# Two pairs of convolution-gate tiles by seven quarter products, with the attention work moved ahead of them

## The chip, the cores and the metric

The kernel runs on one core of one Trainium2 chip. A core has a matmul engine (TensorE, PE in the profile; its weight loads are PEld), a vector engine (VectorE, DVE), a scalar engine (ScalarE, ACT), GpSimd (POOL), and SyncE (SP), which issues most DMAs. The metric is the device time of one execution in microseconds. The kernel before takes 994.15 us (median of three runs, 994.03 to 994.83).

## The reference

One decoder layer over a prompt of 512 tokens and 64 sample tokens (8 sequences of 8), all in float32, width 1024. Cut to what the change touches:

```
h = rmsnorm(x, norm1_g) * (1 + sc1) + sh1
proj = h @ w_in                      # columns: B, C, x (1024 each), q, k, v, gates ga, gb
u = c_gate * xa                      # C * x
uc, new_conv = causal_conv(u, conv_buf, conv_w)      # width 3
ya = (b_gate * uc) @ w_conv_out
o = attend(q, k, v, sinks)           # window 128, 4 kv heads of 64, 16 query heads, ALiBi, sinks
yb = o @ w_attn_out
mixed = sigmoid(ga) * ya + sigmoid(gb) * yb
x = x + g1 * (mixed @ w_mix_out)     # then norm, ConvFFN, residual, final norm
```

`sc1, sh1, g1, ...` come from `silu(c) @ w_ada + b_ada`. Prompt and sample tokens share the weights. The prompt attends to its own previous 128 positions; a sample sequence attends to a cache of 128 keys and its own 8.

## The kernel before

**Layout.** Activations lie transposed, channels on the 128 partitions and the 512 + 64 tokens along the row, eight such tiles for 1024 channels. A column tile of a weight is 1024 x 128, loaded as one tile `raw` of 128 x 8 x 128 (512 KB). float32 is kept by splitting: `hi` is the operand rounded to a short format, by ScalarE (`whi<-raw` for weights), and `lo` the rest, by VectorE (`wlo<-raw,whi`). A product is then hi x hi + hi x lo + lo x hi. `product` (line 228) does one column tile: 8 k-steps, each three passes over two token groups of 256 and 320, which is 48 matmuls into one of two double PSUM tiles `mm`.

**Pairs.** `pair_product` (line 367) does two column tiles at once by seven products of a quarter in place of eight (each of 4 k-steps, three passes, 288 tokens: 84 matmuls). Its operands are sums and differences of halves: of weights in `pair_weights` (316), which gives steps `sums1`, `ah`, `al` and so on that `in_turn` (362) hangs behind the parts of the pair before; of activations in `PairOperands` (255) with `sums`, `high`, `low`, `n3`. In before the two gates (eight pairs, `sigmoid_pair`, 1245), the mixing product and the FFN use pairs; the convolution's B, C, x do not.

**The order of the work around the change.** First the queries and keys of head 0, then the convolution loop over eight channel tiles m: products C(m), x(m), B(m), written below as C0, x0, b0. C times x goes into `pad`, GpSimd copies state out of it, ScalarE and VectorE make the three taps `y`, and `conv_times` multiplies B by `y` into `cy`, which is split into `gh`, `gl`. In rounds m = 1 to 3 `key_parts` and `queries` (805) of the next heads stand ahead of C(m). `queries` makes a product, splits it, and moves its low half to the other 64 partitions by GpSimd's DMA queue (`q<-low`, line 821). Then `state_out`, eight products with `w_conv_out` (`conv_out`), the eight gate pairs, the products with `w_attn_out`, and the rest.

**The filler.** Smaller work is written as a generator and set between k-steps: `tick` (201) adds a rate for each k-step, and for each whole number one step of the generator is issued. Through the convolution loop it is `beside_conv` (1200): first `attention` (1062), 16 pieces (4 heads x 4 blocks of 128 tokens). Round n issues the values of piece n-2 (`prompt_values`, copied out by ScalarE at line 1057 as `o<-aux`), the transposes of piece n-1 (`prompt_turn`, copied at 1040) and the scores of piece n (`prompt_scores`), then the softmax (890: VectorE, and ScalarE's exponentials at 900). `prompt_ready` holds a head's first round back until eight k-steps after its queries. Decode follows for two quarters of the cache (`decode_scores`, `decode_values`), then `modulation(2048)` (1156): four groups of 16 small matmuls (`aux<-ada,cT`, line 1149) from eight loads `ada` of 256 KB each. Its loads go on SP's queue, in order with the weights.

**Who sets the order.** TensorE runs in program order throughout. The other engines' orders are set by a scheduler that estimates durations, until the line `pinned += [pe, act, dve]` ahead of the gates, from which ScalarE and VectorE are in program order too. Pools limit what can be early: four `raw`, five each of `whi` and `wlo`, 57 slots of a general pool, four PSUM banks `aux` for all small products, two double banks `mm`. In `w_split_adding` (168), used in before for six weights of the FFN, the low part is made by ScalarE (minus the high part) and a DMA of GpSimd's queue that adds `raw`.

Of the kernel before, what the change touches and what calls it, by code (L numbers as in the profile page):

```python
# [16 lines left out]
P = 128  # L17
# [12 lines left out]
Q_TICKS = 8  # L30
CACHE_AT = 15, 16
EPS = 1e-6
NEG = -1e33
# [38 lines left out]
def step_kernel(ctx: ExitStack, tc: tile.TileContext, ins: dict, outs: list):  # L72
# [57 lines left out]
    def sv(t):  # L130
        return t[:, 512:576]
# [795 lines left out]
    def decode_scores(q, s, cV):  # L927
# [38 lines left out]
        yield False  # L966

    def decode_values(q, s, cV):
        pt = []
        for kt in range(2):  # L970
# [7 lines left out]
            pt.append(t)  # L978
            yield False
        yield False  # L980
        c = slice(512 + 32 * q, 512 + 32 * q + 32)
        for j in range(2):
            O = aux()
            matmul(O, vt(4)[:, j * P : j * P + P], pt[1], start=True, stop=False)
            p4 = pt[0].rearrange("p (h b r) -> p h b r", h=4, b=4)
            o4 = O.rearrange("p (h b r) -> p h b r", h=4, b=4)
            for b in range(4):
                matmul(
                    o4[:, :, b, :], cV[b // 2][:, b % 2, j * P : j * P + P], p4[:, :, b, :],
                    start=False, stop=(b == 3),  # L990
                )
            oX = slot("oX", shape=[P, 2, 32])
            for hf in range(2):
# [9 lines left out]
                nc.sync.dma_start(dst[HALF[1 - hf]], oX[HALF[hf]])  # L1003
            yield False

# [56 lines left out]
    def attention():  # L1062


        scored = turned = None
        for n in range(18):
            arg = (n // 4, n % 4) if n < 16 else None
# [14 lines left out]
            yield False  # L1082
        filler[1] = 0.5
        waiting = None
# [114 lines left out]

    def beside_conv():  # L1200
# [6 lines left out]
    gcv = []  # L1207
    for m in range(NK):
        if m in (5, 6):
# [21 lines left out]
        nc.scalar.copy(c_sb, ps)  # L1231
        ps = product(weights(kpm(w_in, 2048 + m * P), NK), h)
        u = padded()
# [5 lines left out]
        y = conv(u, parT[:, 64 + m : 65 + m], parT[:, 72 + m : 73 + m], parT[:, 80 + m : 81 + m], stT[:, m, :])  # L1239
        ps = product(weights(kpm(w_in, m * P), NK), h)  # L1240
        gcv.append(split_slot(conv_times(ps, y), "g"))
    state_out(NK, ncv_p[:], ncv_s[:])
# [22 lines left out]

    ya, made = [], {}
    wco, wao = ins["w_conv_out"][0], ins["w_attn_out"][0]
    gate_cols = [c + m * P for c in (4608, 5632) for m in range(0, NK, 2)]
# [17 lines left out]
    w_last = weights(kpm(wco, (NK - 1) * P), NK)  # L1286
    gate_raws(0)
    pinned += [pe, act, dve]
    w, steps = pair_weights(*raws[0])
    steps = in_turn(steps)  # L1290
    for n in sorted(steps):
        steps[n]()
    gate_raws(1)
    conv_out(NK - 1, w_last)
    drain()
    sg, o = [], []
    w_next = {}

# [10 lines left out]
    for n in range(len(gate_cols)):  # L1309
# [7 lines left out]
        else:  # L1317
# [636 lines left out]
```

## Time and profile before

| | us |
|---|---|
| median of three runs | 994.15 (994.03 to 994.83) |
| profiled execution | 995.13 |
| its span | 993.4 |
| TensorE busy, share | 977.9, 98% |
| VectorE busy, share | 688.8, 69% |
| ScalarE busy, share | 464.6, 47% |
| GpSimd busy, share | 103.7, 10% |
| granted TensorE clock, mean | 0.996 |

The span is what the profiler saw from the first to the last instruction; the execution's own time lies 1.7 us above it. In the trace the convolution loop runs from 65 to 323 us, the products with `w_conv_out` to 382, the gate pairs to 471 and the products with `w_attn_out` to 532. Helpers record every operation under one line (111 in before, 112 in after), so groups are told apart by the names of their tiles: `mm<-hh,whi` is a pass of a product of the activations h, `aux<-kh,q` are prompt scores, `aux<-ident,s` transposes of softmax rows, `aux<-pt,V` values. Idle time in the list of waits is put down to what came last. A matmul's records overlap, since the engine is pipelined, so what one costs is read from start to start.

### The profile page before, as it was taken

Reading aid. Unit: us, or ns where it says so; the run is one execution under the profiler, and the core shown is the slowest. Engines: PE = TensorE matmul, PEld = TensorE weight load, DVE = VectorE, ACT = ScalarE, POOL = GpSimd, SP = SyncE. Lnnn points to the kernel's source line nnn. Section 1 sums busy time; section 2 is a strip of 40 time slices with the busy share of each in tenths; the row PEclk is TensorE's granted clock in tenths of the full one; section 3 lists DMA queues with packets and bytes.
Section 4 is the critical chain, followed back from the end, with each engine's and each line's share of the span. In section 5 each row is a group of like instructions: output and inputs, shape, how many; then the busy total and the mean of one; then the engine's idle time right before and its main releaser. Section 6 shows DMA issues by size and latency. Waiting matters only on the chain.

```text
span 993.4 us, 18735 instructions
## 1 busy us (share of the span) xinstructions
PE 977.9 (98%) x7492; PEld 939.1 (95%) x7492; DVE 688.8 (69%) x1289; ACT 464.6 (47%) x861; POOL 103.7 (10%) x275
## 2 busy tenths in 40 slices
PE   7999999999999999999999999999999999999997
PEld 5899999999999989999889999999999999999997
DVE  5736776676452348888578778896569994579853
ACT  5454555555334325454334468653225552245453
POOL 2221101020100000000000032111001110001120
PEclk9999999999999999999999999999999999999999
DMA  9984332243422753234962543433232232323302
GB/s 298 320 245 113 85 87 74 86 116 108 145 68 65 238 191 86 85 86 129 342 221 70 146 110 85 108 102 91 85 107 85 86 89 83 107 77 100 101 10 96
DMA packets 174345, 122.33 MB, mean 123 GB/s; under 512 B 6983, under 2 KB 160942, under 8 KB 173970
## 3 DMA queue, kind: packets, MB, share of 16 engines
q1 hardware_dynamic: 170242, 109.36, 36.3%
q0 software_dynamic: 3872, 11.51, 4.6%
q8 instruction: 59, 0.97, 0.4%
q14 instruction: 28, 0.23, 0.1%
q10 hardware_dynamic: 144, 0.26, 0.1%
HBM read 109.17 MB, written 7.35 MB: 117 GB/s over the span
## 4 chain that ended last, share of the span: by engine, by line
PE 88%; DVE 4%; DMA 3%; issue 2%; ACT 1%; SPq 0%; POOL 0%; POOLq 0%; DVEq 0%; ACTq 0%
PE mm L111 63%; PE aux L111 22%; PE aux L1049 2%; PE aux L1149 1%; DMA ad<-in_w_ada 1%; DVE wlo L111 1%; DMA wlo<-raw 1%; DMA raw<-in_w_in 1%; SPq L418 0%; DVE uv L111 0%; DVE raw L111 0%; DVE y L111 0%; DVE cy L111 0%; ACT whi L111 0%; DVE fl L111 0%
## 5 line engine op out<-in xcount | busy, mean ns | idle before, releaser
L111 ACT ACTIVATE whi<-raw 128x1024 fp32r<-128x1024 f32 (+2 forms) x166 | 170.2, 1034 | 150.6 <-PE mm L111 80.6
L111 DVE TENSOR_TENSOR wlo<-raw,whi 128x1024 fp32r<-128x1024 f32 (+2 forms) x160 | 190.4, 1193 | 47.3 <-ACT whi L111 46.8
L111 PE MATMUL mm<-hh,whi 128*128 128x256 f32 (+2 forms) x560 | 124.7, 299 | 0.6 <-ACT hh L111 0.6
L111 PE MATMUL mm<-hh,wlo 128*128 128x256 f32 (+2 forms) x560 | 121.8, 294 | 0.0
L111 PE MATMUL mm<-hl,whi 128*128 128x256 f32 (+2 forms) x560 | 121.1, 295 | 0.0
L111 PEld LDWEIGHTS mm<-hh,whi 128*128 128x128 f32 x560 | 93.1, 188 | 2.9 <-ACT hh L111 1.2
L111 PEld LDWEIGHTS mm<-hh,wlo 128*128 128x128 f32 x560 | 94.2, 188 | 0.0
L111 PEld LDWEIGHTS mm<-hl,whi 128*128 128x128 f32 x560 | 93.6, 188 | 0.4 <-DVE hl L111 0.4
L111 PE MATMUL mm<-th,whi 128*128 128x288 f32 x224 | 66.6, 297 | 0.4 <-DVE uv L111 0.4
L111 PE MATMUL mm<-th,wlo 128*128 128x288 f32 x224 | 66.1, 295 | 0.0
L111 PE MATMUL mm<-tl,whi 128*128 128x288 f32 x224 | 66.0, 295 | 0.0
L111 PE MATMUL mm<-fl,whi 128*128 128x256 f32 (+1 forms) x304 | 65.2, 295 | 0.0
L111 PE MATMUL mm<-fh,whi 128*128 128x256 f32 (+1 forms) x304 | 64.8, 295 | 0.3 <-DVE rt L111 0.3
L111 PE MATMUL mm<-fh,wlo 128*128 128x256 f32 (+1 forms) x304 | 65.0, 295 | 0.0
L111 DVE SCALAR_TENSOR_TENSOR x<-mm,modT,x 128x512 f32<-128x512 f32 (+1 forms) x29 | 19.6, 676 | 57.7 <-PE mm L111 57.7
L111 PEld LDWEIGHTS mm<-fh,whi 128*128 128x128 f32 x304 | 50.8, 188 | 0.5 <-PE mm L111 0.5
L111 PEld LDWEIGHTS mm<-fl,whi 128*128 128x128 f32 x304 | 50.9, 188 | 0.0
L111 PEld LDWEIGHTS mm<-fh,wlo 128*128 128x128 f32 x304 | 50.9, 188 | 0.0
L900 ACT ACTIVATE s<-s,nmx 128x256 f32<-128x256 f32 (+1 forms) x72 | 34.0, 475 | 32.0 <-DVE nmx L897 31.2
L111 PE MATMUL aux<-2h,whi 128*128 128x288 f32 (+2 forms) x160 | 47.3, 296 | 0.0
L111 PE MATMUL aux<-2l,whi 128*128 128x288 f32 (+2 forms) x160 | 47.3, 295 | 0.0
L111 PE MATMUL aux<-2h,wlo 128*128 128x288 f32 (+2 forms) x160 | 47.2, 295 | 0.0
(332 smaller groups left out, 2610.7 us busy)
## 6 DMA issues: line engine op xcount, KB each, us to landing
raw<-in_w_in SPq DMA_DIRECT2D x52, 512.0 KB, 4.2
raw<-in_w_up SPq DMA_DIRECT2D x44, 512.0 KB, 3.9
ada<-in_w_ada SPq DMA_DIRECT2D x64, 256.0 KB, 5.7
ad<-in_w_ada SPq DMA_DIRECT2D x32, 256.0 KB, 6.3
raw<-in_w_down SPq DMA_DIRECT2D x16, 512.0 KB, 3.6
raw<-in_w_conv_out SPq DMA_DIRECT2D x8, 512.0 KB, 3.5
raw<-in_w_attn_out SPq DMA_DIRECT2D x8, 512.0 KB, 4.7
raw<-in_w_mix_out SPq DMA_DIRECT2D x8, 512.0 KB, 5.1
```

The source lines that it names most:

```text
L111: done = getattr(self.engine, name)(*args, **kwargs)
L900: nc.scalar.activation(s[x // 2][:, x % 2, :w], s[x // 2][:, x % 2, :w], AF.Exp, bias=nmx[:, x : x + 1], accum_out=den[:, x : x + 1],)
L1049: done = nc.tensor.matmul(O[HALF[par], :256], vt(i - nkt + 1 + kt)[:, hd * 64 : hd * 64 + 64], pts[kt][:, par * 256 : par * 256 + 256], st ...
L1149: done = nc.tensor.matmul(ps[32 * j : 32 * j + 32, :], cT[:, k, :], cols[k][j], start=(k == 1), stop=(k == NK - 2),)
```

## The change

- B's last four column tiles (m = 4 to 7) leave the loop. They are made after it as two pairs by `pair_product`: `b_pair`. Their `y` are kept until then. The pair operands of h, which before were made beside `conv_out`, are made in the loop, m = 4 to 7, and their last part in the first B pair.
- Attention's rate is 0.24 for 0.19, decode's 0.35 for 0.5; the rest of both is issued at the end of the loop, ahead of the pairs. Between a piece's scores and its transposes there is one more round. `key_parts` and `queries` of the next heads stand between C(m) and x(m), m = 0 to 2. x's weights are prepared ahead of the copy of C.
- In the convolution loop weights from C3 on (eleven) take their low parts by `w_split_adding`.
- `decode_scores` issues both halves of a quarter in one step. `decode_values` uses for each of its two outputs only the half of the columns that belongs to it, in one bank, in one step.
- ScalarE and VectorE are in program order from the B pairs on. The weights of `w_conv_out` are prepared two products ahead, the weight steps of the first gate pair are spread over `conv_out` m = 3 to 6, and `modulation(2048)` moves from there to beside the gate pairs, its rest issued before the last of these.

```diff
+ATT_RATE, ADDING_FROM, B_PAIRS = 0.24, 3, (4, 6)
...
 decode_scores
-            for hf in range(2):
-                hd = 2 * j + hf
+        for j in range(2):
+            for hf in range(2):
+                hd, at = 2 * j + hf, j * 256
...
-            yield False
+        yield False
...
 decode_values
+        O = aux()
         for j in range(2):
-            O = aux()
-            matmul(O, vt(4)[:, j * P : j * P + P], pt[1], start=True, stop=False)
+            hs = slice(2 * j, 2 * j + 2)
+            own = slice(j * 256, j * 256 + 256)
+            matmul(O[:, own], vt(4)[:, j * P : j * P + P], pt[1][:, own], start=True, stop=False)
             for b in range(4):
                 matmul(
-                    o4[:, :, b, :], cV[b // 2][:, b % 2, j * P : j * P + P], p4[:, :, b, :],
+                    o4[:, hs, b, :], cV[b // 2][:, b % 2, j * P : j * P + P], p4[:, hs, b, :],
...
 attention
-        for n in range(18):
+        for n in range(19):
...
-            turned = (*scored[:2], prompt_turn(*scored)) if scored else None
-            scored = (*arg, []) if arg else None
+            turned = (*waiting[:2], prompt_turn(*waiting)) if waiting else None
+            waiting, scored = scored, (*arg, []) if arg else None
...
-        filler[1] = 0.5
+        filler[1] = 0.35
...
-        filler[1] = 13 / 76
-        yield from modulation(2048)
...
-    fill(beside_conv(), 0.19)
+    fill(beside_conv(), ATT_RATE)
+    ops = [PairOperands(h, kp, made) for kp in range(4)]
+    def conv_w(c0):
+        raw = load_w(kpm(w_in, c0), NK)
+        if len(gcv) + len(ys) < ADDING_FROM:
+            return split_w(raw)
+        w, low = w_split_adding(raw)
+        low()
+        return w
     for m in range(NK):
-        if 1 <= m <= 3:
-            key_parts(m)
-            for t in (2 * m, 2 * m + 1):
-                queries(t)
-        ps = product(weights(kpm(w_in, 1024 + m * P), NK), h)
+        ps = product(conv_w(1024 + m * P), h)
+        if m == NK - 2:
+            raws = [load_w(kpm(w_in, (B_PAIRS[0] + j) * P), NK) for j in range(2)]
+            w_pair, steps = pair_weights(*raws)
+            steps = in_turn(steps)
+        w = conv_w(2048 + m * P)
+        if m == NK - 1:
+            for n in (2, 3, 4):
+                steps[n]()
...
+        if m < 3:
+            key_parts(m + 1)
+            for t in (2 * m + 2, 2 * m + 3):
+                queries(t)
+        if m >= NK - 4:
+            ops[m - NK + 4].sums()
+            ops[m - NK + 4].high()
+        ps = product(w, h)
...
+        if m >= NK - 4:
+            ops[m - NK + 4].low()
+        if m == NK - 2:
+            steps[0]()
+        if m < B_PAIRS[0]:
+            ps = product(conv_w(m * P), h)
+            gcv.append(split_slot(conv_times(ps, y), "g"))
+        else:
+            ys[m] = y
+    drain()
+    pinned += [act, dve]
...
+    def b_pair(m, w, steps):
+        ya, yb, n = ys.pop(m), ys.pop(m + 1), 512 - HT
+        ta, tb = slot("cy"), slot("cy")
...
+        pair_product(w, made["op"], steps, a0, later(ta, ya), b0, later(tb, yb))
+        return ta, tb
...
+    for m in B_PAIRS:
+        parts = [{0: lambda: [op.n3() for op in ops]}] if m == B_PAIRS[0] else [{4: g_split}]
+        if m != B_PAIRS[-1]:
+            raws = [load_w(kpm(w_in, (m + 2 + j) * P), NK) for j in range(2)]
+            after, t = pair_weights(*raws)
+            parts.append(in_turn(t))
+        else:
+            raw = [load_w(kpm(wco, j * P), NK) for j in range(2)]
+            parts.append({n: lambda j=j: w_next.update({j: split_w(raw[j])}) for j, n in ((0, 2), (1, 3))})
+        done = b_pair(m, w_pair, merged(*parts))
...
-    for m in range(NK - 1):
-        w = weights(kpm(wco, m * P), NK)
-        if m >= 3:
-            PairOperands(h, m - 3, made).all()
-        conv_out(m, w)
...
+    for m in range(NK):
+        conv_out(m, w_next.pop(m))
+        if m + 2 < NK:
+            w_next[m + 2] = weights(kpm(wco, (m + 2) * P), NK)
+        if m >= 3 and steps:
+            steps.pop(min(steps))()
...
+        if n == 0:
+            fill(first_modulation(), 13 / 120)
         if n + 1 == len(gate_cols):
+            drain()
             fill(modulations(), 2 / 28)
```

More of the change, by code (lines that the diff above doesn't have):

```diff
@@ L1003, in decode_values @@
                 nc.sync.dma_start(dst[HALF[1 - hf]], oX[HALF[hf]])
-            yield False
+        yield False
     def prompt_ready(hd, i):
@@ L1198, in modulations, with first_modulation @@
         yield True
+    def first_modulation():
+        yield from modulation(2048)
+        yield True
     def beside_conv():
         yield from attention()
-        filler[1] = 13 / 76
-        yield from modulation(2048)
         yield True
-    fill(beside_conv(), 0.19)
-    gcv = []
+    fill(beside_conv(), ATT_RATE)
+    wco, wao = ins["w_conv_out"][0], ins["w_attn_out"][0]
+    gcv, ys, made = [], {}, {}
+    ops = [PairOperands(h, kp, made) for kp in range(4)]
[6 more added lines that the diff above has]
+        return w
     for m in range(NK):
@@ L1231, in step_kernel @@
         nc.scalar.copy(c_sb, ps)
-        ps = product(weights(kpm(w_in, 2048 + m * P), NK), h)
+        if m < 3:
[6 more added lines that the diff above has]
+        ps = product(w, h)
         u = padded()
@@ new lines, in step_kernel, with merged, a0, b0 @@
+    drain()
+    pinned += [act, dve]
+    def merged(*parts):
+        out = {}
+        for at in range(8):
+            fs = [p[at] for p in parts if at in p]
+            if fs:
+                out[at] = lambda fs=fs: [f() for f in fs]
+        return out
+    def b_pair(m, w, steps):
+        ya, yb, n = ys.pop(m), ys.pop(m + 1), 512 - HT
+        ta, tb = slot("cy"), slot("cy")
+        def a0(ps):
+            dve.tensor_tensor(out=ta[:, :HT], in0=ps, in1=ya[:, :HT], op=ALU.mult)
+        def b0(x, y, op):
+            dve.tensor_tensor(out=tb[:, :HT], in0=x, in1=y, op=op)
+            dve.tensor_tensor(out=tb[:, :HT], in0=tb[:, :HT], in1=yb[:, :HT], op=ALU.mult)
+        def later(t, yy):
+            def done(x, y, op):
+                dve.tensor_tensor(out=y, in0=x, in1=y, op=op)
+                dve.tensor_tensor(out=t[:, HT:512], in0=y[:, :n], in1=yy[:, HT:512], op=ALU.mult)
+                nc.gpsimd.tensor_tensor(
+                    out=b8(sv(t)), in0=b8(y[:, n:]), in1=b10(yy)[:, :, 0:8], op=ALU.mult
+                )
+            return done
+        pair_product(w, made["op"], steps, a0, later(ta, ya), b0, later(tb, yb))
+        return ta, tb
@@ new lines, in step_kernel, with g_split @@
+    before, w_next = [], {}
+    def g_split():
+        for t in before:
+            gcv.append(split_slot(t, "g"))
+        before.clear()
+    for m in B_PAIRS:
[8 more added lines that the diff above has]
+        done = b_pair(m, w_pair, merged(*parts))
+        before += done
+        w_pair = after if m != B_PAIRS[-1] else None
@@ L1242, in step_kernel @@
+    g_split()
     state_out(NK, ncv_p[:], ncv_s[:])
@@ L1279, in conv_out @@
         ya.append(t)
-    for m in range(NK - 1):
-        w = weights(kpm(wco, m * P), NK)
-        if m >= 3:
-            PairOperands(h, m - 3, made).all()
-        conv_out(m, w)
-    w_last = weights(kpm(wco, (NK - 1) * P), NK)
     gate_raws(0)
-    pinned += [pe, act, dve]
     w, steps = pair_weights(*raws[0])
     steps = in_turn(steps)
[L1291 to L1295, printed above, removed]
+    for m in range(NK):
[4 more added lines that the diff above has]
+            steps.pop(min(steps))()
+            if not steps:
+                gate_raws(1)
     sg, o = [], []
-    w_next = {}
     def part_o(n):
```

14 lines of the change are left out of this document (6 added, 8 removed).

## The prediction

> **What bounds the kernel now.** I read the page's busy times and its chain of waits first, then the table by stretches, then single pieces of the timeline.
>
> ```profile
> span 993.4 us, 18735 instructions
> PE 977.9 (98%) x7492; PEld 939.1 (95%) x7492; DVE 688.8 (69%) x1289; ACT 464.6 (47%) x861; POOL 103.7 (10%) x275
> PE 88%; DVE 4%; DMA 3%; issue 2%; ACT 1%; SPq 0%; POOL 0%; POOLq 0%; DVEq 0%; ACTq 0%
> ```
>
> TensorE is busy for 98% of the span and is 88% of the chain that ended last. So the time is the sum of the matmuls in their order, and two things move it: matmuls that go, and instants at which TensorE waits for something new. The rows by stretches (columns: span, PE, PEld, DVE, ACT, POOL, clock, DMA share, GB/s) show one stretch inside the attention work and one of gate pairs alone.
>
> ```profile
> 100.00:150.00 50.00, 50.00 (x381) 46.29 (x380) 35.40 (x92) 26.80 (x67) 6.58 (x15) 1.00 0.33 89
> 400.00:450.00 50.00, 50.00 (x379) 50.00 (x379) 41.83 (x61) 24.45 (x40) 0.00 (x0) 1.00 0.35 99
> ```
>
> PE has no gap in either and the granted clock is 1.00. In the second every matmul is 288 columns wide: 50.00 / 379 = **0.132 us** each, weight load included. A matmul pair of 256 and 320 columns has the same mean width, so I price it at 2 x 0.132.
>
> **The change part by part.**
>
> *Two pairs by seven products.* Four column tiles of B took 4 x 8 k-steps x 3 passes x 2 groups = 192 matmuls of 288 columns in the mean; two pairs take 2 x 7 x 4 x 3 = 168 of 288. 24 go: 24 x 0.132 = **-3.2 us**.
>
> *Halved decode values.* The timeline of one of the four pieces in before (start, duration of the group, x count of records):
>
> ```profile
> 304.40 1.02 PE L111 MATMUL aux<-pt,V 128*128 128x512 f32 x2
> 305.25 1.05 PE L111 MATMUL aux<-pt,cKV 128*128 128x128 f32 x8
> 306.06 0.52 PE L111 MATMUL mm<-hh,whi 128*128 128x256 f32 x2
> 584.90 0.80 PE L111 MATMUL aux<-ones,acc 128*128 128x2 f32 x6
> 585.56 0.36 PE L111 MATMUL mm<-2h,whi 128*128 128x256 f32 x1
> ```
>
> The product with V takes 305.25 - 304.40 = 0.85 us for 512 columns. Four of them at 256 columns save 4 x 0.43 = **-1.7**. The products with the cache take 0.81 / 8 = 0.101 per record of 128 columns. At 64 columns they could save 32 x 0.05 = -1.6 if columns alone counted. But the ones,acc group, two columns wide, takes (585.56 - 584.90) / 6 = 0.110 a record: below some width the columns cost nothing. I take 0, the value of that row, and keep -1.6 as the other end. The Trainium skill ("TensorE: Matmul & The Clock Gate", LDWEIGHTS) gives a weight load as the number of its columns over 1.2, 107 ns for 128, whatever moves past it; the trace agrees with 101 to 110 ns, and by its gap formula without the weight load (section Back-to-back issue gap) the halves would save more. The sum above does without either.
>
> *Fewer interruptions.* Decode scores come in one piece a quarter of the cache, not two:
>
> ```profile
> 280.94 0.43 PE L111 MATMUL mm<-hh,wlo 128*128 128x256 f32 x2
> 281.30 0.45 PE L111 MATMUL aux<-kTc,qS 64*32 64x128 f32 x16
> 282.10 0.53 PE L111 MATMUL mm<-hh,whi 128*128 128x256 f32 x2
> 282.46 0.42 PE L111 MATMUL mm<-hl,whi 128*128 128x256 f32 x2
> 282.73 0.43 PE L111 MATMUL mm<-hh,wlo 128*128 128x256 f32 x2
> ```
>
> A pair of matmuls takes 0.27 (282.46 to 282.73), the one before the piece 0.36 and the one behind it 0.36: 0.2 a visit. Two visits go: **-0.4**. The joined pieces of the values may give as much again; the nineteenth round of attention takes 0.2 back. Dense work: -3.2 - 1.7 - 0.4 = **-5.3 us**.
>
> *First scores sooner.* Attention now runs at 0.24 pieces a k-step, not 0.19, and queries(2) stands behind C0. In the changed order the first scores follow one k-step of the product behind C0, not three: 12 matmuls, 1.6 us, sooner. What they need comes over POOL's queue:
>
> ```profile
> 77.11 0.52 POOL L821 DMA_DIRECT2D q<-low  x1 [5.37 <-DVE low L817]
> 77.95 0.52 POOL L821 DMA_DIRECT2D q<-low  x1 [0.32 <-issue]
> 81.62 0.28 PE L111 MATMUL aux<-kh,q 128*128 128x256 f32 x1
> ```
>
> ```profile
> DMA to landing us min/median/max: 4.0/4.0/4.0
> ```
>
> ```profile
> DMA to landing us min/median/max: 3.8/3.8/3.8
> ```
>
> These are the landings of the two transfers: 77.11 + 4.0 = 81.1 and 77.95 + 3.8 = 81.7. Nothing ahead of them changes on any engine. The scores would start at 80.0, run 0.5 on the two heads that are there, wait to 81.1 and, after 0.24, to 81.7: 0.6 + 0.4 = **+1.0** (0.6 to 1.1).
>
> *Scores behind ScalarE's queue.* A piece of prompt attention takes five banks (values, two transposes, two scores), and there are four: the second scores take the bank of the values, so TensorE waits there for ScalarE's copy of them (line 1057). In before that never bites:
>
> ```profile
> 100.65 0.65 PE L1049 MATMUL aux<-pt,V 128*64 128x256 f32 x4
> 102.64 0.28 PE L111 MATMUL aux<-kh,q 128*128 128x256 f32 x1
> 101.51 0.35 ACT L1057 COPY o<-aux 128x256 f32<-128x256 f32 x1
> 107.30 0.51 ACT L900 ACTIVATE s<-s,nmx 128x256 f32<-128x256 f32 x1 [3.21 <-DVE nmx L897]
> 109.38 1.05 ACT L111 ACTIVATE whi<-raw 128x1024 fp32r<-128x1024 f32 x1
> 110.46 1.21 ACT L814 ACTIVATE q<-mm 64x512 fp32r<-64x512 f32 x2
> ACT o L1057 <- PE aux L1049: 28.2, 14, 4.0
> ```
>
> ScalarE stood idle before 14 of the 16 copies (28.2 us, up to 4.0). In after two steps a piece at 0.24 a k-step make 8.3 k-steps of 0.79 us, 6.6, and with 2.5 of its own a piece comes every 9.1 us, not 10.8; and eleven weights get their low part by a second ScalarE pass. In the piece inside x1 ScalarE has, from the end of the product before (which frees the buffer of a high part): whi 1.05, exponentials 109.38 - 107.30 = 2.08, two q copies 1.21, the copy 0.35, together 4.7, and some 0.4 of handing over. TensorE is at the second scores after 18 matmuls (2.4) and 102.64 - 100.65 = 2.0: 4.4. It waits 0.7 to 0.8. By the same count b2's piece (two weight passes, y, the copy) waits about 1.0, C3's 0.7, b3's 0.4, q7's 0.1: 3.0. In the others the copy has slack, if ScalarE ran as closely as I count. Such counts leave out that an instruction may be ready earlier, so I take half, **+1.6** (0 to 3.0; 8 if ten pieces lost 0.8, below). Nothing else than the second scores is queued behind this wait, and everything on TensorE behind those.
>
> *modulation(2048) beside the gate pairs.* It moves 32 loads of 256 KB behind SP's gate weights, one group of matmuls every 54 to 57 matmuls (7.5 us) and 1.0 of its own. In before the groups beside conv_out stood further apart; the second modulation, beside attn_out, has 48 matmuls (6.3 us) between groups, in both kernels. All waits of the two modulations for loads are in this answer for the tile ada, releaser, us, times:
>
> ```profile
>   DMA ada<-in_w_ada: 0.6, 2
> DMA to landing us min/median/max: 2.9/5.7/7.1
> ```
>
> So I take **+0.6**, that row; 0 if the wider distance suffices, and 2.7 if three groups each wait 0.9 because the gate weights ahead of them on SP hold for a buffer.
>
> *At nothing, with their cover.* The eleven adds by DMA have three to four products, 20 us and more, to land; before's six took:
>
> ```profile
> wlo<-raw POOLq DMA_DIRECT2D x6, 512.0 KB, 5.9
> PEld mm L111 <- DMA wlo<-raw: 0.7, 1, 0.7
> ```
>
> One came 0.7 late: the price of each if the cover goes. They are queued on POOL between the q transfers (0.52 each to issue) and ahead of pad and state copies, which have a product to spare. VectorE, in turn, is relieved of nine low parts. The pair operands move from conv_out into the conv loop and cost VectorE and ScalarE the same work in another place. By the stretch of gate pairs a pair gives VectorE 84% of 84 x 0.132 = 11.1 us, 9.3; the first B pair adds four low parts of n3 and four multiplications by y, so VectorE may just pass 11.1. Decode's last values (0.85 + 16 x 0.10 = 2.5 us on TensorE among it) cover that: 0, up to +1.0 if not. Queries behind C, key parts, weights two ahead: the same loads in about the same distance, 0. Sums1 of the first gate pair is spread over conv_out, where VectorE is at half load: 0.
>
> **Sum.** -5.3 + 1.0 + 1.6 + 0.6 = -2.1. The profiled execution took 995.13 us, 1.0 above the median 994.15. 995.13 - 2.1 = 993.0, and on the scale of the median **992.0 us**.
>
> **The rivals.**
>
> 1. *No new wait but the first.* ScalarE is 54% busy in the stretch of attention above, and idle before the copies; the forecast's other waits may not come. -5.3 + 1.0 = -4.3: **989.9**; 988.3 if the halves of the cache save too.
> 2. *ScalarE's queue becomes the pace of attention* (slower). If exponentials, weight passes and copies follow each other without slack in ten of sixteen pieces, each second scores waits as in x1, 0.8: +8.0 in place of 1.6, -5.3 + 1.0 + 0.6 + 8.0 = +4.3: **998.4**. It decides from the point at which more than about 4.4 us of ScalarE work lies between a product's end and the copy. For it: a buffer of a high part comes free only at a product's end, so up to 2.1 us of weight passes stand there. Against it: ScalarE was idle before 14 of 16 copies, and the extra round between scores and transposes gives the exponentials longer.
> 3. *The adds come late* (slower). With three products' lead that needs a queue that stands still. VectorE's scaling by the denominators has these rows:
>
> ```profile
> L910 DVE TENSOR_SCALAR s<-s,den 128x256 f32<-128x256 f32 x56 | 16.0, 349 | 0.5
> L910 DVE TENSOR_SCALAR s<-s,den 128x128 f32<-128x128 f32 x16 | 3.5, 281 | 0.1
> ```
>
> 128 columns more take 68 ns, 0.53 ns a column. Eleven times 0.7 on the forecast: -2.1 + 7.7 = +5.6: **999.7**. The Trainium skill ("SBUF — State Buffer", on the trap in which DVE blocks a DMA) says that VectorE's two-port modes lock GpSimd out, so that descriptors of a DMA issued by GpSimd wait; that speaks against putting adds beside softmax, and 0.53 ns a column may be such a mode. By the rows, though, one such instruction lasts 0.35 us, against 20 us of lead.
> 4. *The halves don't shorten V's products* (the change doesn't do what it says there): if the time of the product were not its columns, -2.1 + 1.7 = -0.4: **993.7**.
>
> **How the numbers follow.** A measurement of this kernel can tell about 0.2%, 2.0 us, from no change: faster is below 992.2, slower above 996.1. The forecast 0.42 (its own bounds, waits of 1.4 to 5.6, give 990.2 to 994.4: half of it faster, half within), rival 1 0.24, rival 2 0.20, rival 3 0.08, rival 4 0.06. Faster: 0.22 + 0.23 = 0.45. Slower: 0.18 + 0.08 = 0.26. Within: the rest, 0.29. The range reaches from 988.8, between rival 1 and its lower end, to 998.4, rival 2; what lies beyond is rival 3, part of rival 2 and the end of rival 1, under 0.2 together.
>
> **What would show it.** Counts: 24 fewer product matmuls, V's records at about 0.21 us. At the first scores a wait of TensorE for a q transfer of 0.6 and 0.4. In the waits, TensorE's scores held by ScalarE's copy of line 1057's kind: 1.6 in all for the forecast, none for rival 1, 8 for rival 2; weight loads held by wlo<-raw for rival 3, by ada<-in_w_ada for the modulation. If the cache products shrink below 0.1 a record, the low end is right. If the stages behind 472 us change in length by more than 0.5, a step is missing here.

## The result and the profile after

The changed kernel takes **991.52 us** (median of six runs, 989.63 to 992.42); the kernel before, in the same rounds, 994.62 (six runs, 994.03 to 995.21). The ratio is 0.9966, with a 95% interval of 0.9956 to 0.9976: faster by 2.4 to 4.4 us. 992.0 was predicted, so the sum held to half a microsecond. Several of its terms did not hold, as the next sections show; that they balanced is luck. The profiled execution took 992.42 (before: 995.13).

The page of the changed kernel, its first lines and the chain:

```profile
span 990.6 us, 18761 instructions
PE 973.0 (98%) x7468; PEld 934.7 (94%) x7468; DVE 687.1 (69%) x1300; ACT 477.4 (48%) x880; POOL 118.1 (12%) x290
PE 88%; issue 4%; DMA 3%; DVE 3%; ACT 1%; POOL 1%; SPq 0%; POOLq 0%; DVEq 0%; ACTq 0%
```

PE is 88% of the chain as before, and its records are 24 fewer (7468 for 7492). ScalarE has 12.8 us more work, GpSimd 14.4. Now the starts of three stages, before and after: the first product with `w_conv_out`, the first with `w_attn_out`, the first of the mixing (timeline rows, start, duration).

```profile
323.39 0.51 PE L111 MATMUL mm<-gh,whi 128*128 128x256 f32 x2
471.83 0.43 PE L111 MATMUL mm<-oh,whi 128*128 128x256 f32 x2
532.21 0.43 PE L111 MATMUL mm<-mxh,whi 128*128 128x256 f32 x2
```

```profile
319.47 0.51 PE L112 MATMUL mm<-gh,whi 128*128 128x256 f32 x2
469.18 0.43 PE L112 MATMUL mm<-oh,whi 128*128 128x256 f32 x2
529.43 0.42 PE L112 MATMUL mm<-mxh,whi 128*128 128x256 f32 x2
```

The convolution with attention ends 3.9 us sooner; 1.3 of it is lost again until 469 us, in the stretch through which modulation(2048) moved, from beside the products with `w_conv_out` to beside the gate pairs; nothing changes in the next stage, and the span ends 2.7 sooner (993.4 to 990.6, 2.8 by the rounded figures). What TensorE waits for in the changed kernel (releaser, us in total, times, longest; the first stages left out):

```profile
PE aux L1155 <- DMA ada<-in_w_ada: 1.1, 1, 1.1
...
PE mm L112 <- DMA wlo<-raw: 0.5, 1, 0.5
...
PE aux L112 <- DMA wlo<-raw: 0.4, 1, 0.4
```

The first is the modulation's, at 413 us. The other two are adds of the FFN, past 560 us, which the change doesn't touch; before had one of 0.4 there. No wait of a matmul is put down to ScalarE's copy of line 1063 (line 1057 in before); one weight load's is, 0.2.

The decode values of a quarter, the piece that the halving made:

```profile
283.90 0.59 PE L112 MATMUL aux<-pt,V 128*128 128x256 f32 x2
284.33 1.00 PE L112 MATMUL aux<-pt,cKV 128*128 128x64 f32 x8
285.17 0.65 PE L112 MATMUL aux<-pt,V 128*128 128x256 f32 x2
285.66 1.00 PE L112 MATMUL aux<-pt,cKV 128*128 128x64 f32 x8
286.47 0.51 PE L112 MATMUL mm<-hh,whi 128*128 128x256 f32 x2
```

V's product takes 284.33 - 283.90 = 0.43 and 0.49, for 0.85 before. The cache's takes 0.84 and 0.81 for eight records of 64 columns, before 0.81 for eight of 128: half the columns, the same time.

### The profile page after: what moved, and what is told of

Read it like the earlier page. It is cut to its first block, busy times and chain, and to the rows that moved or that the text cites. A ratio compares the mean times of both kernels' runs of the same rounds, so it can differ in the third digit from the quotient of the medians.

```text
span 990.6 us, 18761 instructions
## 1 busy us (share of the span) xinstructions
PE 973.0 (98%) x7468; PEld 934.7 (94%) x7468; DVE 687.1 (69%) x1300; ACT 477.4 (48%) x880; POOL 118.1 (12%) x290
## 4 chain that ended last, share of the span: by engine, by line
PE 88%; issue 4%; DMA 3%; DVE 3%; ACT 1%; POOL 1%; SPq 0%; POOLq 0%; DVEq 0%; ACTq 0%
PE mm L112 63%; PE aux L112 23%; PE aux L1055 2%; PE aux L1155 2%; DMA wlo<-raw 1%; DMA x<-in_x_prompt 1%; DVE wlo L112 1%; DMA ada<-in_w_ada 1%; POOL wlo L112 0%; SPq L419 0%; DVE uv L112 0%; DVE raw L112 0%; DVE ol L112 0%; ACT junk L112 0%; ACT oh L112 0%
## 5 line engine op out<-in xcount | busy, mean ns | idle before, releaser
L112 DVE TENSOR_TENSOR wlo<-raw,whi 128x1024 fp32r<-128x1024 f32 (+2 forms) x151 | 179.3, 1192 | 68.3 <-ACT whi L112 67.9
L112 PE MATMUL mm<-hh,whi 128*128 128x256 f32 (+1 forms) x504 | 113.0, 299 | 0.6 <-ACT hh L112 0.6
L112 PE MATMUL mm<-hh,wlo 128*128 128x256 f32 (+1 forms) x504 | 110.5, 294 | 0.0
L112 PE MATMUL mm<-hl,whi 128*128 128x256 f32 (+1 forms) x504 | 109.6, 294 | 0.0
L112 PEld LDWEIGHTS mm<-hh,whi 128*128 128x128 f32 x504 | 84.0, 188 | 2.7 <-ACT hh L112 1.3
L112 PEld LDWEIGHTS mm<-hh,wlo 128*128 128x128 f32 x504 | 85.0, 188 | 0.0
L112 PEld LDWEIGHTS mm<-hl,whi 128*128 128x128 f32 x504 | 84.5, 188 | 0.4 <-DVE hl L112 0.4
L112 PE MATMUL mm<-tl,whi 128*128 128x288 f32 x240 | 70.9, 295 | 0.0
L112 POOL DMA_DIRECT2D wlo<-raw x17 | 15.0, 884 | 293.4 <-PE mm L112 233.3
L112 PEld LDWEIGHTS mm<-th,whi 128*128 128x128 f32 x240 | 45.2, 188 | 2.5 <-issue 2.5
```

The costliest lines, as they stand in the source:

```text
L112: done = getattr(self.engine, name)(*args, **kwargs)
```

## The experiments

Each kernel was timed in rounds with the kernel before, on one chip for each group; the ratio is to before. The change itself stands at 0.9966 (0.9956 to 0.9976).

| kernel | median us | before us | ratio | 95% |
|---|---|---|---|---|
| before, decode part of the change alone | 992.86 | 994.86 | 0.9982 | 0.9973 to 0.9990 |
| change, pairs undone, n3 ahead | 998.78 | 994.86 | 1.0039 | 1.0027 to 1.0051 |
| change, pairs undone, n3 behind | 995.67 | 994.49 | 1.0007 | 0.9998 to 1.0016 |
| change, modulation at 13/180 | 991.40 | 994.86 | 0.9966 | 0.9954 to 0.9978 |
| change, attention at 0.32 | 993.99 | 994.86 | 0.9993 | 0.9984 to 1.0001 |
| change, no adds by DMA | 992.40 | 994.49 | 0.9980 | 0.9971 to 0.9989 |
| change, no extra round | 995.61 | 994.76 | 1.0008 | 0.9998 to 1.0018 |
| change, first scores later and modulation at 13/140 | 990.71 | 994.49 | 0.9959 | 0.9946 to 0.9971 |
| the same, no adds | 990.27 | 994.76 | 0.9951 | 0.9933 to 0.9968 |
| three pairs, attention 0.28 | 999.09 | 994.49 | 1.0044 | 1.0032 to 1.0057 |
| three pairs, waits taken out | 990.06 | 994.76 | 0.9952 | 0.9937 to 0.9968 |
| three pairs, waits taken out, no adds | 989.96 | 994.76 | 0.9950 | 0.9934 to 0.9965 |

The theory: time is TensorE's sum, the change takes some 5 us of matmuls and visits out of it, and a few waits give part back. The rivals: the gain comes from the moves and not from the pairs; ScalarE's queue, or the adds, set the pace.

**The decode part alone.** `decode_scores` and `decode_values` of the change, put into before; nothing else.

```diff
-            matmul(O, vt(4)[:, j * P : j * P + P], pt[1], start=True, stop=False)
+            matmul(O[:, own], vt(4)[:, j * P : j * P + P], pt[1][:, own], start=True, stop=False)
...
-            yield False
+        yield False
```

> Before, with only the decode part of the change: halved and joined decode values, decode scores of both halves in one step. My theory (the time is the sum of the matmuls): V's products save about 1.5 and the fewer interruptions 0.4, the cache's halves nothing, so 1.9 less than before, about 992.7 us, with no new wait. The rival that the halves save nothing: within 0.4 of before. If the cache's halves saved by their columns: 3.5 less.

Measured: 992.86 for 994.86, 2.0 less (by the interval 1.0 to 2.7). The theory holds, and the cache's halves save nothing here either: in this trace, too, a group of eight takes 0.84 and 0.81.

**The pairs undone, first try.** Four products of eight k-steps behind the loop, in place of two pairs:

```diff
-    for m in B_PAIRS:
-        parts = [{0: lambda: [op.n3() for op in ops]}] if m == B_PAIRS[0] else [{4: g_split}]
...
+    for n, m in enumerate(range(B_PAIRS[0], NK)):
+        if n == 0:
+            w0, w1 = b_w
+            [op.n3() for op in ops]
+        ps = product(w0, h)
...
+        gcv.append(split_slot(conv_times(ps, ys.pop(m)), "g"))
```

> The change with B's last four column tiles as four products of eight k-steps at the same place, behind the loop, in place of two pairs; all else stays. My theory: 24 matmuls of 0.132 come back, 3.2 more than the change, about 994.7. The rival that the gain is from the moved attention and the decode part: under 1 more. A rival that the pairs cost VectorE time which TensorE waits for: the products would give up less than 3.2, and the change's trace would show waits in the two pairs.

Measured: 998.78, 7.3 above the change. But n3 overwrites half of four tiles of h, and the products here read those tiles afterwards: they multiply other values than the reference's, and the first of them waits for the new ones, 298.37 - 296.28 = 2.1 us for one matmul:

```profile
296.28 0.36 PE L112 MATMUL mm<-hh,whi 128*128 128x256 f32 x1
298.37 0.42 PE L112 MATMUL mm<-hh,whi 128*128 128x320 f32 x1 [1.72 <-ACT hh L112]
```

So this run doesn't price the pairs. The next does.

**The pairs undone, n3 behind the last product.**

```diff
-            [op.n3() for op in ops]
         ps = product(w0, h)
+        if m == NK - 1:
+            [op.n3() for op in ops]
```

> The change with B's last four column tiles as four products behind the loop, as in the run before, but with the last part of the pair operands (n3, which overwrites half of four tiles of h) behind the last of these products and not ahead of the first. My theory: the 24 matmuls cost 3.2, so about 994.7, and no wait at the first product. The rival that the pairs bring little and the rest of the change carries the gain: under 992.5.

Measured: 995.67, ratio 1.0007: without the pairs the whole change is no faster than before. Against the change that is 0.41%, 4.1 us. In the traces, summing start to start over all product passes (with no interval counted as more than 0.4, so that long waits drop out) gives 3.4 us more for these 24 matmuls (0.14 each); another 0.7 is a wait at the first scores that this execution had and the change's profiled one had not (below). The pairs, then, are the larger part of the gain. They and the decode part would make -2.0 - 3.4 = -5.4, and -3.1 came: the rest of the change costs 2.3. Some 2 us of waits that before had not are in the change's profiled execution: 1.1 at ada, 0.3 inside the scores, and 0.5 more at the adds of the FFN, which the change doesn't touch.

**Modulation spread wider.**

```diff
-            fill(first_modulation(), 13 / 120)
+            fill(first_modulation(), 13 / 180)
```

> The change with modulation(2048) spread wider beside the gate pairs (13 steps in 180 k-steps, not 120). My theory: the one wait of 1.1 for ada in the profiled execution goes, 0.5 to 1.1 less in the median, about 990.7. The rival that the loads are held by the weights ahead of them on SP's queue whatever the distance: no change, the wait at a later group.

Measured: 991.40, no different. The wait for ada is gone from the list, but another has come (PE, timeline; the last column is idle time and releaser), and one that was small is large:

```profile
80.21 0.28 PE L112 MATMUL aux<-kl,q 128*128 128x256 f32 x1
81.24 0.36 PE L112 MATMUL aux<-kh,q 128*128 128x256 f32 x1 [0.76 <-DMA q<-low]
81.44 0.28 PE L112 MATMUL aux<-kl,q 128*128 128x256 f32 x1
81.75 0.36 PE L112 MATMUL aux<-kh,q 128*128 128x256 f32 x1
...
436.23 0.29 PE L112 MATMUL aux<-hh,wlo 128*128 128x288 f32 x1
437.42 0.37 PE L112 MATMUL mm<-th,whi 128*128 128x288 f32 x1 [0.90 <-DVE uv L112]
```

At 437.42 a gate pair's sixth part waits for VectorE, 1.2 start to start where 0.13 is usual. VectorE had stood idle 6.36 us before the weight part `wl<-s,wh`, and ScalarE 7.25 before the high part it follows: the wider spread holds eight slots of the general pool for longer, which fits, but it was not tested by itself. The rival's forecast, no change, was right here; its mechanism, loads held by the weights ahead of them and a wait at a later group, does not show, since no group waits for ada.

At 80.21 stands the first scores' wait of the prediction: 81.24 - 80.21 is 1.03 where 0.12 is usual, and 81.75 - 81.44 is 0.31. That is 1.1 in this execution, 0.9 in that of the pairs undone, and 0.1 in the change's profiled one. The two transfers in this trace, and in the change's own:

```profile
77.60 0.52 POOL L822 DMA_DIRECT2D q<-low  x1 [6.06 <-DVE low L818]
78.44 0.52 POOL L822 DMA_DIRECT2D q<-low  x1 [0.32 <-DVE snks L864]
```

```profile
77.01 0.52 POOL L822 DMA_DIRECT2D q<-low  x1 [4.82 <-DVE low L818]
77.85 0.52 POOL L822 DMA_DIRECT2D q<-low  x1 [0.32 <-DVE snks L864]
```

```profile
80.48 0.28 PE L112 MATMUL aux<-kh,q 128*128 128x256 f32 x1
81.07 0.28 PE L112 MATMUL aux<-kl,q 128*128 128x256 f32 x1
81.24 0.36 PE L112 MATMUL aux<-kh,q 128*128 128x256 f32 x1
```

```profile
DMA to landing us min/median/max: 3.6/3.6/3.6
```

```profile
DMA to landing us min/median/max: 3.3/3.3/3.3
```

In the change's trace they landed at 80.6 and 81.2, by scores that come at 80.48 and reach the last head at 81.2: just in time. Here they took no longer, 3.5 and 3.2 us, but went out 0.6 later, while the scores came at 79.85, 0.6 sooner. With the pairs undone they went out at 76.69 and 77.53, took 4.3 and 3.9, and the scores came at 79.97. So not only the landing varies, but also when the transfer goes out and when TensorE comes to it.

**Attention faster.**

```diff
-ATT_RATE, ADDING_FROM, B_PAIRS = 0.24, 3, (4, 6)
+ATT_RATE, ADDING_FROM, B_PAIRS = 0.32, 3, (4, 6)
```

> The change with attention at 0.32 steps a k-step, not 0.24: a piece every 6.3 k-steps, 7.4 us with its own work, not 9.1. The theory that ScalarE's queue decides: the second scores wait for ScalarE's copy in many pieces, 2 to 8 us more, and the list of waits names ACT o. The rival that its slack is ample: within 1 of the change.

Measured: 993.99, 2.5 above the change. The trace has three waits of TensorE inside scores, of 0.8, 1.0 and 1.0 beyond the usual 0.12 (at 108.5, 173.7 and 195.5 us). The second, with VectorE's and ScalarE's rows beside it:

```profile
173.74 0.28 PE L112 MATMUL aux<-kl,q 128*128 128x256 f32 x1
174.86 0.39 PE L112 MATMUL aux<-kh,q 128*128 128x256 f32 x1 [0.84 <-DVE s L1029]
```

```profile
174.06 0.75 DVE L1029 SCALAR_TENSOR_TENSOR s<-con,aux 128x256 f32<-128x256 f32 x2 [1.75 <-PE aux L112]
```

```profile
174.63 0.35 ACT L1063 COPY o<-aux 128x256 f32<-128x256 f32 x1
```

It looks like rival 2's wait, but it is not: ScalarE's copy ends at 174.98, after the scores went on. VectorE's reading of the first scores ends at 174.06 + 0.75 = 174.81, and 0.05 later they go on. In the compiled kernel the two score tiles of this piece, and of the one at 108.5, lie in one and the same bank: the pool gave the second the bank of the first and not that of the values (why was not tested, and no row here shows banks). So the shortage of banks is what costs (five tiles, four banks), but the reader waited for is VectorE. The third wait is for the last head's q transfer:

```profile
190.70 0.97 POOL L112 DMA_DIRECT2D wlo<-raw  x1
191.28 0.93 POOL L822 DMA_DIRECT2D q<-low  x1
196.58 0.39 PE L112 MATMUL aux<-kh,q 128*128 128x256 f32 x1 [0.82 <-DMA q<-low]
```

It is issued right behind one of the adds on GpSimd's queue and lands 5.3 us later. In every trace with adds such a transfer takes 4.5 to 5.3; the other transfers of the last head, in all traces, take 2.1 to 4.3. So what is queued right behind an add lands later. At 0.24 nothing waited for that; here it is one of the three waits. This kernel was not run without adds at 0.32. The forecast number held (2 to 8) with another cause than the one forecast: no wait here is ScalarE's.

**No adds by DMA.**

```diff
-ATT_RATE, ADDING_FROM, B_PAIRS = 0.24, 3, (4, 6)
+ATT_RATE, ADDING_FROM, B_PAIRS = 0.24, 99, (4, 6)
```

> The change without the eleven adds by DMA: VectorE makes these low parts, as in before. My theory (TensorE waits for neither): within 0.5 of the change. The rival that VectorE, 61% busy in the loop and with the pair operands on top, falls behind: 1 to 4 more, with waits of TensorE for DVE. The rival that ScalarE's second passes cost the change something: 0.5 less.

Measured: 992.40, ratio 0.9980 for 0.9966: between the theory and its rival. In the profiled execution no wait for VectorE's low parts appears; the wait for ada is 1.8 and not 1.1, and the span is the change's to 0.1 (990.6). In the two later comparisons, the kernels with both waits taken out and those with three pairs, leaving out the adds makes the time 0.4 and 0.1 less. No effect of the adds on the time is shown either way.

**Both waits taken out.**

```diff
-Q_TICKS = 8
+Q_TICKS = 10
...
-            fill(first_modulation(), 13 / 120)
+            fill(first_modulation(), 13 / 140)
```

> The change with both of its waits taken from their place: a head's first scores ten k-steps behind its queries, not eight (the first scores then come behind three k-steps, as in before), and modulation(2048) at 13 steps in 140 k-steps. Theory of the two waits: 0 to 1.1 less for the first, up to 1.1 for the second, about 990.2. The rival that such waits move on to another place: no less than 991.0.

Measured: 990.71, five runs within 0.5 of each other (990.42 to 990.89), ratio 0.9959; the change's own six spread over 2.8. In its trace the first scores follow each other at 0.12 (83.39 to 84.33), and neither ada nor a q transfer is among the waits. 0.8 less than the change, of the forecast 1.3. The intervals of the two ratios overlap, so the gain over the change is likely and not shown. No run has one edit alone, but in the traces the modulation's brings nothing: from the second part of the first gate pair to the first product with `w_attn_out` the change takes 97.21 us (371.97 to 469.18) and this kernel 97.22 (370.96 to 468.18). The wait for ada is gone, and the scheduler has cut a group of the modulation in two:

```profile
385.36 1.05 PE L1155 MATMUL aux<-ada,cT 128*32 128x512 f32 x4
388.14 1.91 PE L1155 MATMUL aux<-ada,cT 128*32 128x512 f32 x12
```

The two parts take 1.0 and 1.8 us, a whole group 1.85 (394.78 to 396.63 in the change). So the rival holds for this edit: a cost of the same size stands in the wait's place. Of the 1.6 between the two spans 1.0 lies ahead of the gate pairs and 1.1 between the mixing and the FFN's first `mm<-fh,whi`, where neither edit acts (last section); 0.5 comes back in other places.

**The same without adds.**

```diff
-ATT_RATE, ADDING_FROM, B_PAIRS = 0.24, 3, (4, 6)
+ATT_RATE, ADDING_FROM, B_PAIRS = 0.24, 99, (4, 6)
```

> The kernel with both waits taken out, without the adds by DMA. TensorE waited for neither ScalarE's nor VectorE's low parts there, so within 0.7 of it, 990.7. The rival that the adds relieve VectorE where it counts: 1 or more above.

Measured: 990.27, 0.4 from 990.71. Who makes the low parts doesn't show in the time at this rate.

**No extra round.**

```diff
-        scored = waiting = turned = None
-        for n in range(19):
+        scored = turned = None
+        for n in range(18):
...
-            turned = (*waiting[:2], prompt_turn(*waiting)) if waiting else None
-            waiting, scored = scored, (*arg, []) if arg else None
+            turned = (*scored[:2], prompt_turn(*scored)) if scored else None
+            scored = (*arg, []) if arg else None
```

> The change without the extra round between a piece's scores and its transposes, as in before. My theory (ScalarE's queue, not the softmax's length, sets how fast attention can go at 0.24): transposes of a piece then come 8.3 k-steps, 9 us, behind its scores, and the softmax takes under 9, so within 1 of the change. The rival that the round is what keeps the copies from being late: waits of TensorE for the softmax (DVE s or ACT s at the transposes), 3 or more.

Measured: 995.61, 4.1 above the change: the rival was right and I was not. The transposes wait for the softmax:

```profile
143.20 1.08 PE L1055 MATMUL aux<-pt,V 128*64 128x256 f32 x8
146.01 0.76 PE L112 MATMUL aux<-ident,s 128*128 128x128 f32 x2 [1.72 <-DVE s L911]
```

They wait 2.1 us here (ahead of the first transpose and behind the second) and 0.2 at 97 us; a B pair waits 0.4 for VectorE. Up to the first product with `w_conv_out` this execution is 2.6 us behind the change's (322.09 for 319.47). The rest of the difference lies behind it, where the edit changes nothing: the wait for ada is 1.7, and two adds of the FFN were 0.7 and 0.3 late. At 0.24 a round is 9 us, and a softmax behind two queues, VectorE's and ScalarE's, takes longer than that in at least one piece. So the extra round is part of what lets attention end in time; without it the kernel is no faster than before, though of the 4.3 between the two profiled executions only the 2.6 lie where the edit acts.

**Three pairs.** B's last six tiles, with attention and decode faster so that they end ahead of the pairs:

```diff
-ATT_RATE, ADDING_FROM, B_PAIRS = 0.24, 3, (4, 6)
+ATT_RATE, ADDING_FROM, B_PAIRS = 0.28, 3, (2, 4, 6)
...
-        filler[1] = 0.35
+        filler[1] = 0.5
```

> The change with three pairs (B's last six column tiles), attention at 0.28 and decode at 0.5 steps a k-step so that all of it ends ahead of the pairs. Matmuls alone: 12 fewer, 1.6 less than the change, 989.9. The theory that ScalarE's queue decides what attention can bear: at 0.28 between the change (no such wait) and 0.32 (three waits of 0.8 to 1.0), 1 to 2 back, so 990.5 to 992.

Measured: 999.09, a miss by 7. One wait of 0.9 is for ScalarE's copy, as forecast (223 us, named in the list); two others decide. The second decode transposes came too soon behind their softmax,

```profile
278.99 0.42 PE L112 MATMUL mm<-hh,wlo 128*128 128x256 f32 x2
282.67 0.50 PE L112 MATMUL aux<-ident,s 128*128 128x128 f32 x2 [3.27 <-DVE s L911]
```

and the first scores, sooner still, waited 2.2 for their q transfers. Less 0.4 at ada and the 1.6 of matmuls, that makes 4.4 of the 6.1 between the two profiled executions. Another 1.5 is the clock. Right behind the first scores' wait TensorE's granted clock is 0.50 for 3.4 us, as this row of the stretch from 84 to 85 us shows (columns as in the prediction, the clock third from the end):

```profile
84.00:85.00 1.00, 1.00 (x6) 1.00 (x6) 0.14 (x1) 0.99 (x5) 0.37 (x1) 0.50 1.19 225
```

Nine pairs of product matmuls, from 82.57 to 86.59 us, take 4.0 where 2.5 is usual. All five runs of this kernel have a mean granted clock of 0.994 or 0.995, the change's 0.996 or 0.997. That the wait brings the lower clock is not shown: behind the longer wait at 279 us it stays at 1.00. Some 0.5 is in the pairs, behind VectorE's `uv`. The two large waits are settings of rates, so they were mended.

**Three pairs, waits taken out.**

```diff
+ATT_RATE, ADDING_FROM, B_PAIRS = 0.29, 3, (2, 4, 6)
+Q_TICKS = 10
+        filler[1] = 0.4
+            fill(first_modulation(), 13 / 140)
```

> Three pairs again, with what the last run's waits named taken out: first scores ten k-steps behind their queries, decode at 0.4 (30 matmuls between the second decode scores and their transposes, as in the change), attention at 0.29, modulation(2048) at 13 in 140. Matmuls: 1.6 less than the kernel with both waits taken out (990.7), 989.1. The theory of ScalarE's queue: one or two waits of 0.8 to 1.0 for line 1063's copy, so 989.5 to 991. The rival that the third pair costs something of its own beside VectorE: over 992.

Measured: 990.06, within the forecast. It is 0.65 below the kernel with both waits taken out, where 1.6 of matmuls went, with overlapping intervals: a gain of the third pair by itself is not shown. One wait at the second scores is left of any size, and here it is ScalarE's copy (177.73 to 178.10 in its rows):

```profile
177.30 0.28 PE L112 MATMUL aux<-kl,q 128*128 128x256 f32 x1
178.15 0.38 PE L112 MATMUL aux<-kh,q 128*128 128x256 f32 x1 [0.57 <-ACT o L1063]
```

**Three pairs, no adds.** The edit is again 99 in place of 3.

> The run before (three pairs) without the adds by DMA: nine fewer ScalarE passes in the loop. If ScalarE's queue is what holds the second scores: fewer such waits, 0 to 1.5 less than that run. If VectorE then becomes late (the pair operands and low parts together): more, with waits for DVE.

Measured: 989.96, the lowest of all, 4.8 below before (0.9950, 0.9934 to 0.9965), 0.1 below the run with adds. The wait of 0.7 at 177 us is gone, as the theory of ScalarE's queue has it for this wait, but the time shows no difference. (The trace of the run with adds has ten of them, so ten passes went, not the nine of the expectation.) Both three-pair kernels beat before clearly; with the change itself the intervals overlap (up to 0.9968 and 0.9965, from 0.9956).

## Why the prediction was right, and which steps were not

1. *24 matmuls, -3.2.* Right: 24 records fewer, and 3.4 by the run without pairs. Between before and the change the same sum over the product passes is 3.6 lower, which holds fewer interruptions too.
2. *Decode values, -1.7, cache halves nothing.* Right: V's records save 0.42 and 0.36 by the rows above, and as much again in the other quarter, 1.6; the cache's are unchanged. The column count that would have given -1.6 more was rightly set aside for the row of ones,acc.
3. *Interruptions, -0.4.* Right in the run with the decode part alone (2.0 in all). In the change it can't be told apart. Its trace has 69 visits of small work between product passes, before 74, the decode part alone 68, so all but one of the visits stay saved; the 0.4 by which the sum of the passes exceeds 3.2 fits them, but that sum scatters by some 0.3 between executions.
4. *First scores, +1.0.* The mechanism was right, the size varies: 0.1 in the change's profiled execution, 0.9 and 1.1 in two others with the same order there. I had taken the landings of one execution, 4.0 and 3.8 us, and the scores at 80.0; the next had 3.6 and 3.3, and 80.48, and there the wait is nearly nothing. "Nothing ahead of them changes" held for the order of the work, not for its times.
5. *Second scores behind ScalarE, +1.6.* This step failed in size (its 1.6 is called half of 3.0, which is 1.5). In x1's piece, the one counted in the prediction, the change's trace has:

```profile
139.28 1.06 ACT L112 ACTIVATE whi<-raw 128x1024 fp32r<-128x1024 f32 x1 [4.05 <-PE mm L112]
142.31 1.18 ACT L815 ACTIVATE q<-mm 64x512 fp32r<-64x512 f32 x2
143.51 0.37 ACT L1063 COPY o<-aux 128x256 f32<-128x256 f32 x1
```

```profile
139.35 0.43 PE L112 MATMUL mm<-hh,whi 128*128 128x256 f32 x2
143.68 0.28 PE L112 MATMUL aux<-kl,q 128*128 128x256 f32 x1
143.94 0.39 PE L112 MATMUL aux<-kh,q 128*128 128x256 f32 x1
```

   ScalarE's chain from 139.28 to 143.88 is 4.6 us, the 4.7 of the prediction. What was wrong is "some 0.4 of handing over": the high part starts 0.07 us ahead of the next product, not 0.4 behind the end of the last, since a product's final pass reads only the low part and frees the high one's buffer two matmuls early. The wait is 0.14, not 0.8, and the other four pieces show none. A chain of 4.6 against a cover of 4.5 decides at a few tenths; with three pairs and higher rates single pieces crossed that line, by 0.9 (0.28) and 0.7 (0.29).
6. *Modulation, +0.6.* 1.1 in the profiled execution, once: between the 0.6 taken and the bound of 2.7. The second mechanism of the prediction, gate weights on SP that hold for a buffer, is not what SP's queue shows:

```profile
393.25 12.15 SPq L112 DMA_DIRECT2D ada<-in_w_ada  x11
405.49 0.92 SPq L112 DMA_DIRECT2D raw<-in_w_in  x1
406.50 2.63 SPq L112 DMA_DIRECT2D ada<-in_w_ada  x5
```

   Five of the last eight loads are issued from 406.5 on, for a group that stands ready at 413.4. The weight between costs 1.0. But the eleven loads ahead of it take 12.15 us, and they wait for their own kind: in SP's list of waits from 403 to 405.4 us stand 2.3 for an earlier load of ada and 1.3 for the matmuls that still read one.
7. *Adds at nothing.* Right at this rate: for the eleven in the loop the trace has no wait, and taking them out changes the median by +0.9, -0.4 and -0.1 in three comparisons. They landed in 4.4 to 9.1 us (median 4.7), and with some 20 us of lead nothing waits for them. What the step left out is that they hold up a q transfer behind them, the 1.0 at 0.32. The rule of the Trainium skill ("SBUF — State Buffer", on the trap in which DVE blocks a DMA) that spoke for rival 3 may act in the longest; no run here shows whether it does: VectorE was busy for 8.3 of its 9.1 us, but also for 3.6 of the 4.4 of another.
8. *The extra round and the moved attention at nothing beyond their visits.* The cover that the round gives was not priced: the prediction names it only among the arguments against rival 2. Without it the change is 4.1 slower and level with before, of which the softmax's waits are 2.3 in the profiled execution.

So the total came out within half a microsecond by luck, because errors balanced: terms 4 and 5 were 0.9 and 1.5 too high in the profiled execution, term 6 was 0.5 too low, and the FFN's adds (0.5 more than in before) were not in the sum; the rest of the balance is not placed. The mechanism, TensorE's sum and a few waits that give part back, stands, and the two parts of the change that lower the sum were each shown by a run of their own.

## What to carry to other kernels

When one engine is busy for 98% of the time, count its instructions first; then, for each place where work is moved, write down what the bound engine will wait for there, with cover and chain in one currency, and ask above all which buffer is freed by which pass, since a few tenths decide whether a wait exists. Halving a matmul's columns need not halve its time: from 512 to 256 it did here (0.85 to 0.43), from 128 to 64 it saved nothing (0.81 to 0.84 for eight). And a wait that is removed by spreading work can come back at another place (an equal time with another list of waits), so read the list again after every edit. A DMA that nothing waits for can still hold up a small one queued behind it.

## What the runs showed that was not expected

The landing of one and the same transfer of 128 KB differs between executions by a few tenths (4.0 and 3.8 us in before, 3.6 and 3.3 in the change, 4.3 and 3.9 with the pairs undone), and a schedule that meets it to the tenth has a wait of 0.1 to 1.1.

A larger difference lies where no edit acts. From the first matmul of the mixing to the first `mm<-fh,whi` the change takes 148.5 us (529.43 to 677.92), the kernel with both waits taken out 147.4 (528.60 to 675.98). Of the thirteen profiled executions compared here (all but the one in which n3 stands ahead), the eight in which TensorE waits for no add of the FFN take 147.3 to 147.6, the five in which it does (before and the change among them) 148.0 to 148.9. So these adds, which before has too, are late in some executions and not in others, and one profile against another can differ by 1.6 us for that alone.

The change's six runs spread over 2.8 us, the five of the kernel with ten k-steps in place of eight and the modulation wider over 0.5. Which of these waits makes the spread is not shown, since one execution of each kernel is profiled.
